# A transformer-SSD block on one core: more first products among the norms, a second bank for the states, other queues and places

## The chip, the cores and the metric

The kernel runs on one core of a Trainium2 chip. The metric is the device time in microseconds, here the median of three runs. Engines: TensorE (PE) multiplies, VectorE (DVE), ScalarE (ACT) and GpSimd (POOL) work on tiles, SyncE (SP) issues DMAs; ACT and POOL can issue DMAs too. Each has its own queue of instructions.

## The reference

One layer of depth 1 on 1024 tokens of width 1024, in fp32:

```python
f = swiglu(rmsnorm(h, ffn1_pre_g), ffn1_w_gate, ffn1_w_up, ffn1_w_down)   # d_ff 2816
h = h + 0.5 * rmsnorm(f, ffn1_post_g)
m = hybrid_mixer(rmsnorm(h, mix_pre_g))    # 8 heads of differential attention beside 16 heads of
h = h + rmsnorm(m, mix_post_g)             # a two-way Mamba-2 SSD (8 chunks of 128); one w_in, one w_out
f = swiglu(rmsnorm(h, ffn2_pre_g), ffn2_w_gate, ffn2_w_up, ffn2_w_down)
h = h + 0.5 * rmsnorm(f, ffn2_post_g)
return rmsnorm(h, final_g)
```

`swiglu(x)` is `(silu(x @ w_gate) * (x @ w_up)) @ w_down`. The SSD carries one state per group of heads from chunk to chunk: `state = state * decay + B^T (x dt decay)`.

## The kernel before

Every fp32 product is made of three matmuls (`mm3`, line 227): each operand is split into a high part (an ACT cast to the matmul's fp32 type) and a low part (the rest, by a DVE or POOL subtraction; `split`, line 223), and hi x hi, hi x lo and lo x hi are added in one PSUM bank.

The program is written in order, and the order of the instructions on each engine is chosen when it is built, from an estimate of when each is ready. In the chunks of the SSD PE's order is the written one, and in the attention that of PE, ACT, DVE and POOL.

*Gate and up (`blocks_gate_up`, line 368).* The two 1024 x 2816 products of a feed-forward are done in 2 x 2 blocks by a scheme with seven block products instead of eight. The 22 column tiles are taken in 11 pairs (i, i + 11). For a pair and a weight, `matrix` (line 420) loads two raw tiles, makes the sums s1 to s4 on POOL (lines 427 to 430), splits seven half tiles (`unit`), and runs seven `product`s of 12 matmuls (line 386) against the blocks b11, b21, b22, t1 to t4 of the normed tokens. C11 = a11 b11 + a12 b21 is one of the four results, and its first half a11 b11 (called u) enters the other three.

*The beginning of a feed-forward.* `blocks_prep` (line 323) prepares one row tile t of 128 tokens: a square sum on ACT, two small POOL steps (lines 253, 254), a scaling on DVE (line 330), for t >= 4 the sums t1 to t4 with the row tile t - 4 on POOL and DVE (lines 345 to 348), and turns: four PE transposes into one bank, then the split (ACT cast, DVE subtraction). Tiles 0 to 3 give b11 and b21, tiles 4 to 7 give b22, t1, t2, t3 and t4. Only when tile 7 is turned can a product with t2 begin; products with b11 and b21 can begin after tile 3. So `early` runs some of them among the norms: `begun` (line 399) does both products of C11 for gate and up of pair 0 in banks 4 and 5 and keeps u in SBUF, `held` (line 410) does a11 b11 of pair 1 in banks 6 and 7. `matrix` takes over what they left. In the first feed-forward `early` stands at line 1421, raw tiles have three places and split tiles six; in the second at line 1563, among the last rounds of the output projection, with two places each until `grow`.

*The chunks (`ssd_chunks`, line 811).* In chunk c, at step k = 1, the states of the two groups are made by `ssd_state` (line 782): three matmuls into the bank "st", then an addition to sf on DVE (line 792). Between the groups and between all steps stands `next(fill)`: 12 matmuls of the projections of q, k and v (`proj_heads`). Bank "pt" takes the transposes of the finished chunk c - 1 at k = 2 (`turn`, line 915). `decays` (line 852) multiplies dl and dr into two banks "pd"; `ssd_sums` (line 756) loads the rows of dl and dr, three DMAs for each of four groups of heads. For chunk 0 these loads follow the POOL selects of `ssd_rows` (line 754).

*The end of the heads.* Each half of a q or k tile is scaled and split into a tile o (`qk_store`, lines 981 and 982) and stored by SP (line 985); o has two places. After the chunks, the loads of the first attention head are issued on POOL (`attn_first`), the first w_out tile is loaded and split (`out_rounds`, by `unit`, lines 215 and 224), and the last eight steps of the heads run. The memory of that w_out tile was the chunks' before; the last chunk's rows (yT) are stored from it to mixT by ACT's queue (line 925).

Of the kernel before, what the change touches and what calls it, by code (L numbers as in the profile page):

```python
# [189 lines left out]
class Kernel:  # L190
    def __init__(self, ctx, tc, a):
# [6 lines left out]
        self.running, self.early = [], {}  # L198
# [124 lines left out]
    def blocks_prep(self, tags, x, y, ps, gain, C, t, junk=None):  # L323
# [44 lines left out]
    def blocks_gate_up(self, ring, cp, spool, ps, C, wg, wu, gd, early):  # L368
# [30 lines left out]
        def begun(i, banks):  # L399

            def one(r, b):
                p = ps.at(b, [P, 512], "b")
                u = spool.tile([P, 512], F32, tag="u", name="u", bufs=2)
                product(p, unit(r[:, 0:512], G), "b11")
                A.copy(out=u, in_=p)
                product(p, unit(r[:, 512:1024], G), "b21", True)
                first.append((u, p, b))
            return [lambda r=raw(w[i]), b=b: one(r, b) for w, b in zip((wg, wu), banks)]

        def held(i, banks):  # L410

            def one(w, b):
                r = ring.load(1024)[:, 0:512]
                nc.sync.dma_start(out=r, in_=w[i][:, 0:512])
                p = ps.at(b, [P, 512], "b")
                product(p, unit(r, G), "b11")
                first.append((None, p, b))
            return [lambda w=w, b=b: one(w, b) for w, b in zip((wg, wu), banks)]

        def matrix(w, i, final):  # L420
            u, p1, kept = first.pop(0) if first else (None, None, None)
            whole = u is None
# [8 lines left out]
            if not whole:  # L431
                final(i, 0, p1)
                ps.turn.append(kept)
            else:
                u = tile()
                if p1 is None:
                    p1 = bank()
                    product(p1, unit(a11), "b11")
                A.copy(out=u, in_=p1)
# [9 lines left out]
            if whole:  # L449
                product(p1, unit(a12), "b21", True)  # L450
                final(i, 0, p1)
                if kept is not None:
                    ps.turn.append(kept)
# [9 lines left out]
        early(begun, held)  # L463
# [318 lines left out]
    def ssd_state(self, ps, bt, xw, new, first, groups=(0, 1)):  # L782

        for g in groups:
            gs = slice(g * 512, (g + 1) * 512)
            bs = slice(g * P, (g + 1) * P)
            st = ps.tile([P, 512], F32, tag="st", name="st", bufs=1)
# [23 lines left out]
    def ssd_chunks(self, sp, ps, gain, fill):  # L811
# [125 lines left out]
        for s in range(N + 3):  # L937
# [30 lines left out]
            if k == 1 and c < T - 1:  # L968
                self.ssd_state(ps, C[c]["bt"], C[c]["xw"], self.sf, c == 0, (1,))
# [54 lines left out]

    def proj_v(self, ring, qp, ps, halves, g):

        w = [self.unit(ring, self.a["w_v"][g, i], 1024) for i in range(4)]
        for t in range(T):
# [7 lines left out]
            o = qp.tile([P, 2, 512], F32R, tag="o", name="o", bufs=2)  # L1036
# [6 lines left out]
    def proj_qk(self, ring, qp, ps, halves, pair):  # L1043

        for b in range(1, 4):
            w = self.unit(ring, self.a["w_qk"][3 * pair + b - 1], 1024)
            for half in range(2):
# [7 lines left out]
                self.qk_store(qp.tile([P, 2, 512], F32R, tag="o", name="o", bufs=2), p, pair, b, half)  # L1055
# [324 lines left out]
def build(tc, a, out, stages="all"):  # L1380
    nc = tc.nc
    with ExitStack() as top:
# [25 lines left out]
        k.gd = dr([NF, P, S], F32, name="gd")  # L1408
        with ExitStack() as c1:
            ps = Banks(k.pool(c1, "ps1", space=PSUM))  # L1410
            with ExitStack() as cb:
# [9 lines left out]
                def early(begun, held):  # L1421
# [9 lines left out]

                    ps.turn = [0, 1, 2, 3]
# [231 lines left out]
```

## Time and profile before

| | us |
|---|---|
| median of three runs | 2584.19 (2583.44 to 2584.79) |
| profiled execution | 2583.4 |
| its span, first to last instruction | 2581.6 |
| PE busy | 2474.8 |
| DVE busy | 1638.7 |
| ACT busy | 1099.4 |
| POOL busy | 971.7 |

The profile is that of one execution. Busy times are sums over the span; what an engine costs is read where PE stands still. A row of a timeline names start, duration, engine, line and operation, and in brackets how long the engine was idle before it and what ended that.

### The profile page before, as it was taken

The numbers are of one execution on the slowest core, as the hardware profiler recorded it, in microseconds if no ns is written. First come the engines' busy times: TensorE is split into PE (matmuls) and PEld (weight loads), VectorE is DVE, ScalarE is ACT, GpSimd is POOL, SyncE is SP. The second block draws the span as 40 slices with busy tenths as digits, with TensorE's granted clock in tenths as the row PEclk, the third lists the DMA queues.
The fourth block names the chain that finished last, engine by engine and source line by source line (L and its number), as shares of the span: only waits on it lengthen the run. The fifth ranks groups of instructions, "written<-read, shape, count | busy, mean of one in ns | idle before, by whom it ended". The sixth has DMA issues, their size and how long they took to land. (4 is left out here: it accounts for less than half of the span.)

```text
span 2581.6 us, 32800 instructions
## 1 busy us (share of the span) xinstructions
PE 2474.8 (96%) x11904; PEld 2063.1 (80%) x11904; DVE 1638.7 (63%) x2258; ACT 1099.4 (43%) x1899; POOL 971.7 (38%) x853
## 2 busy tenths in 40 slices
PE   6999999999999999999978999999889999999997
PEld 4888888888898889777766888888678888888886
DVE  7656555554746743677636888888875555555655
ACT  5332222343535533454426555555542223224443
POOL 7333231010220294244316666666673323310211
PEclk8999999999999999999999999999889999999999
DMA  4222222756732566465454444442332222227654
GB/s 148 89 74 90 90 74 83 232 182 201 246 121 91 169 214 229 161 198 185 149 163 110 123 119 119 110 122 84 123 102 94 82 86 78 82 91 267 228 167 153
DMA packets 156162, 356.79 MB, mean 138 GB/s; under 512 B 16224, under 2 KB 73696, under 8 KB 151136
## 3 DMA queue, kind: packets, MB, share of 16 engines
q1 hardware_dynamic: 137664, 293.09, 34.2%
q0 software_dynamic: 10016, 57.42, 8.3%
q10 hardware_dynamic: 8320, 4.19, 0.5%
q8 instruction: 94, 1.54, 0.3%
q14 instruction: 68, 0.56, 0.1%
HBM read 263.67 MB, written 90.96 MB: 137 GB/s over the span
## 5 line engine op out<-in xcount | busy, mean ns | idle before, releaser
L225 DVE TENSOR_TENSOR split<-raw,split 128x1024 fp32r<-128x1024 f32 (+3 forms) x223 | 256.1, 1156 | 101.9 <-ACT split L224 101.1
L224 ACT CAST split<-raw 128x512 fp32r<-128x512 f32 (+3 forms) x235 | 190.7, 825 | 191.6 <-issue 86.9
L1117 ACT ACTIVATE e<-sc,st 128x1024 f32<-128x1024 f32 x128 | 143.4, 1120 | 168.9 <-DVE st L1113 168.9
L230 PE MATMUL b<-hT,split 128*128 128x512 f32 x548 | 214.9, 393 | 0.0
L231 PE MATMUL b<-hT,split 128*128 128x512 f32 x548 | 214.3, 391 | 0.0
L232 PE MATMUL b<-hT,split 128*128 128x512 f32 x548 | 214.3, 391 | 0.0
L253 POOL TENSOR_SCALAR rstd<-rstd 128x1 f32<-128x1 f32 x64 | 28.3, 442 | 455.2 <-ACT junk L250 452.8
L231 PE MATMUL po<-split,gs 128*128 128x512 f32 x418 | 165.1, 395 | 0.0
L232 PE MATMUL po<-split,gs 128*128 128x512 f32 x418 | 165.1, 395 | 0.0
L230 PE MATMUL po<-split,gs 128*128 128x512 f32 x418 | 164.4, 395 | 0.0
L230 PE MATMUL pp<-hT,split 128*128 128x512 f32 x384 | 153.8, 400 | 10.4 <-DVE o L982 10.4
L1113 DVE TENSOR_REDUCE st<-sc 128x1 f32<-128x1024 f32 x128 | 150.5, 1217 | 12.6 <-PE sc L1111 12.6
L230 PE MATMUL b<-t,split 128*128 128x512 f32 x396 | 155.4, 392 | 0.1
L231 PE MATMUL b<-t,split 128*128 128x512 f32 x396 | 155.1, 392 | 0.0
L232 PE MATMUL b<-t,split 128*128 128x512 f32 x396 | 154.6, 391 | 0.0
L225 DVE TENSOR_TENSOR gs<-graw,gs 128x384 fp32r<-128x384 f32 (+1 forms) x126 | 70.3, 561 | 132.7 <-ACT gs L224 132.5
L232 PE MATMUL pp<-hT,split 128*128 128x512 f32 x384 | 152.0, 396 | 0.0
L231 PE MATMUL pp<-hT,split 128*128 128x512 f32 x384 | 151.7, 395 | 0.0
L427 POOL TENSOR_TENSOR s<-raw 128x512 f32<-128x512 f32 x31 | 43.6, 1406 | 284.5 <-DMA raw<-in_w_up_dram 143.8
L1124 POOL TENSOR_SCALAR e<-e,st 128x768 f32<-128x768 f32 x64 | 75.7, 1183 | 186.7 <-DVE st L1123 143.0
L224 ACT CAST gs<-graw 128x384 fp32r<-128x384 f32 (+1 forms) x126 | 59.4, 474 | 188.8 <-PE po L232 166.1
L224 ACT CAST split<-s 128x512 fp32r<-128x512 f32 x101 | 60.9, 620 | 142.4 <-PE b L232 131.0
(427 smaller groups left out, 7124.1 us busy)
## 6 DMA issues: line engine op xcount, KB each, us to landing
raw<-in_w_down_dram SPq DMA_DIRECT2D x93, 512.0 KB
acc<-in_w_down_dram SPq DMA_DIRECT2D x39, 512.0 KB
raw<-in_w_gate_dram SPq DMA_DIRECT2D x34, 512.0 KB
raw<-in_w_up_dram SPq DMA_DIRECT2D x32, 512.0 KB
qkd<-o SPq DMA_DIRECT2D x64, 256.0 KB
qk<-qkd POOLq DMA_DIRECT2D x16, 1024.0 KB, 7.8
graw<-gd SPq DMA_DIRECT2D x82, 192.0 KB
gd<-w SPq DMA_DIRECT2D x43, 256.0 KB
```

The lines of the kernel that those rows point to most:

```text
L224: self.nc.scalar.copy(out=hi, in_=src)
L225: (eng or self.nc.vector).tensor_tensor(out=lo, in0=src, in1=hi.bitcast(F32), op=ALU.subtract)
L230: mm(out=out, lhsT=a[0], rhs=b[0], start=start, stop=False, **kw)
L231: mm(out=out, lhsT=a[0], rhs=b[1], start=False, stop=False, **kw)
L232: mm(out=out, lhsT=a[1], rhs=b[0], start=False, stop=stop, **kw)
L253: nc.gpsimd.tensor_scalar(out=r[:, 1:2], in0=r[:, 0:1], scalar1=k / n, scalar2=k * EPS, op0=ALU.mult, op1=ALU.add)
L427: G.tensor_tensor(out=s1, in0=a21, in1=a22, op=ALU.add)
L1113: nc.vector.tensor_reduce(out=X["st"][:, j:j + 1], in_=pc, op=ALU.max, axis=AX.X, negate=True)
L1117: self.nc.scalar.activation(out=X["e", j], in_=X["sc", j], func=AF.Exp, bias=st[:, j:j + 1], accum_out=st[:, 2 + j:3 + j])
L1124: G.tensor_scalar(out=e1[:, XD:], in0=e1[:, XD:], scalar1=st[:, 5:6], scalar2=0.0, op0=ALU.mult, op1=ALU.add)
```

## The change

In both feed-forwards `held` goes, and `begun` does the whole of C11 for pairs 0, 1 and 2: gate and up each with b11 and b21, then silu, multiplication and store. Its u goes to DRAM (`ud`) from POOL's queue, and `matrix` loads it back on SP. In `blocks_prep` the tags in `low` get their low part otherwise: after ACT's cast, PE adds the cast times a negative identity (`minus`) to the transposes' bank, and ACT copies what is left. Those tags are t2, t3, t4 in the first feed-forward and all but b22 in the second. The second group's state uses bank "pt". The dr loads of chunk 0 are issued by ACT. For the last four tiles of the heads, o alternates between its two places and two of the output projection's "odd" tiles.

```diff
+    def new_minus(self, tile):
+        self.minus = tile
+        self.nc.scalar.activation(out=tile, in_=self.ident, func=AF.Copy, scale=-1.0)
...
+    def blocks_prep(self, tags, x, y, ps, gain, C, t, junk=None, low=()):
...
-                nc.tensor.transpose(out=pt[:, i, :], in_=s[:, i * P:(i + 1) * P], identity=self.ident)
-            self.split(pt, C[n][0][:, :, ts], C[n][1][:, :, ts])
+                nc.tensor.matmul(out=pt[:, i, :], lhsT=s[:, i * P:(i + 1) * P], rhs=self.ident, is_transpose=True,
+                                 start=n not in low or i == 0, stop=n not in low or i == 3, skip_group_check=n in low)
+            hi, lo = (c[:, :, ts] for c in C[n])
+            if n in low:
+                nc.scalar.copy(out=hi, in_=pt)
+                nc.tensor.matmul(out=pt, lhsT=self.minus, rhs=hi, start=False, stop=True, skip_group_check=True)
+                nc.scalar.copy(out=lo, in_=pt)
+            else:
+                self.split(pt, hi, lo)
...
         def begun(i, banks):
...
+            ps2 = [ps.at(b, [P, 512], "b") for b in banks]
+            def one(m, w):
+                r = raw(w[i])
                 u = spool.tile([P, 512], F32, tag="u", name="u", bufs=2)
+                product(ps2[m], unit(r[:, 0:512], G), "b11")
+                A.copy(out=u, in_=ps2[m])
+                nc.gpsimd.dma_start(out=ud[2 * i + m], in_=u)
+                product(ps2[m], unit(r[:, 512:1024], G), "b21", True)
+                first.append(2 * i + m)
+            def out():
+                sg = gate11(ps2[0], spool.tile([P, 512], F32, tag="s", name="s", bufs=3))
+                V.tensor_tensor(out=sg, in0=sg, in1=ps2[1], op=ALU.mult)
+                store(sg, i, 0)
+            return lambda: one(0, wg), lambda: one(1, wu), out
...
         def matrix(w, i, final):
+            done = first.pop(0) if first else None
...
+            u = tile()
+            if done is None:
+                p1 = bank()
+                product(p1, unit(a11), "b11")
+                A.copy(out=u, in_=p1)
             else:
+                nc.sync.dma_start(out=u, in_=ud[done])
...
     def ssd_sums(self, c, k):
         dma = self.nc.sync.dma_start
+        right = self.nc.scalar.dma_start if c == 0 else dma
...
-        dma(out=self.dr[32 * k:32 * k + 2].bitcast(F32), in_=src)
+        right(out=self.dr[32 * k:32 * k + 2].bitcast(F32), in_=src)
...
-                    self.ssd_state(ps, C[c]["bt"], C[c]["xw"], self.sf, c == 0, (0,))
+                    self.ssd_state(ps, C[c]["bt"], C[c]["xw"], self.sf, c == 0, (0,), ("st", "pt"))
...
+    def new_o(self, qp):
+        self.os.append(self.os.pop(0))
+        if self.os[-1] is None:
+            return qp.tile([P, 2, 512], F32R, tag="o", name="o", bufs=2)
+        return self.os[-1].tile([P, 2, 512], F32R, tag="odd", name="o", bufs=2)
...
+        k.os = [None, None, wo, wo]
         H = k.attn_first(hp)
```

`early` of the first feed-forward, from tile 4 on (`step` runs one stage of `blocks_prep`):

```diff
-                    gate, up = begun(0, (4, 5))
                     xs += [load(t) for t in (4, 5, 6)]
                     step(4)
                     step(4)
+                    gate, up, out = begun(0, (4, 5))
                     gate()
                     step(5)
+                    step(4)
                     up()
-                    for t in (4, 5, 6, 5, 6):
-                        step(t)
-                    gate, up = held(1, (6, 7))
+                    step(6)
+                    step(5)
+                    step(5)
+                    out()
+                    gate, up, out = begun(1, (6, 7))
                     gate()
+                    step(6)
                     step(7)
                     step(6)
                     up()
                     step(7)
+                    out()
+                    gate, up, out = begun(2, (4, 5))
+                    gate()
                     step(7)
+                    up()
+                    out()
```

`early` of the second, after the last row tile is pushed:

```diff
                 up()
                 k.move()
-                gate, up = held(1, (6, 7))
+                out()
+                gate, up, out = begun(1, (6, 7))
                 gate()
                 k.move()
                 up()
+                out()
                 k.finish()
+                gate, up, out = begun(2, (4, 5))
+                gate()
+                up()
+                out()
```

## Rows read from the trace of the kernel before

**Rows 1.** The page, part 1: busy time of each engine, share of the span, instructions.
```profile
PE 2474.8 (96%) x11904; PEld 2063.1 (80%) x11904; DVE 1638.7 (63%) x2258; ACT 1099.4 (43%) x1899; POOL 971.7 (38%) x853
```

**Rows 2.** Waits of PE, whole span: line <- releaser: us in total, times, longest.
```profile
PE pp L230 <- DVE o L982: 10.4, 1, 10.4
...
PE st L230 <- DVE sf L792: 9.2, 4, 2.4
...
PE pd L856 <- DMA qkd<-o: 4.2, 1, 4.2
...
PE pd L856 <- ACT dd L860: 3.4, 5, 0.7
```

**Rows 3.** Stretches: length, busy PE, PEld, DVE, ACT, POOL (instructions), clock, DMA share, GB/s.
```profile
18.74:41.30 22.56, 22.56 (x113) 18.47 (x112) 13.70 (x16) 9.72 (x18) 21.90 (x21) 0.93 0.32 105
...
41.30:63.98 22.68, 10.29 (x42) 7.60 (x41) 22.55 (x24) 12.82 (x24) 16.94 (x13) 0.60 0.22 70
...
1836.00:1868.74 32.74, 23.11 (x93) 16.91 (x93) 28.27 (x38) 15.62 (x30) 21.39 (x24) 0.84 0.43 150
...
1868.74:1895.80 27.06, 27.06 (x135) 22.09 (x134) 23.38 (x24) 14.54 (x27) 22.86 (x20) 0.94 0.43 148
...
1895.80:1912.70 16.90, 8.73 (x38) 7.08 (x36) 16.46 (x20) 9.93 (x20) 15.42 (x12) 0.60 0.37 120
```

**Rows 4.** Timeline in a chunk (start, duration, engine, line, [idle before]): PE and DVE.
```profile
1159.28 0.39 PE L232 MATMUL pp<-hT,split 128*128 128x512 f32 x1
...
1161.33 0.68 DVE L792 TENSOR_TENSOR sf<-sf,st 128x512 f32<-128x512 f32 x1
...
1162.66 0.63 PE L231 MATMUL st<-xw,bt 128*128 128x512 f32 x1
...
1163.09 0.63 PE L232 MATMUL st<-xw,bt 128*128 128x512 f32 x1
```

**Rows 5.** Timeline at the first chunk's start: POOL, SP's queue and PE.
```profile
1029.36 3.12 POOL L754 TENSOR_SCALAR_AFFINE_SELECT dr<-dr 32x1024 fp32r<-32x1024 f32 x2
...
1034.07 0.25 SPq L760 DMA_DIRECT2D dr<-csT  x1
...
1037.05 1.19 PE L856 MATMUL pd<-dr,dl 128*128 128x512 f32 x2 [4.25 <-DMA qkd<-o]
```

**Rows 6.** Timeline at the end of the heads: ACT.
```profile
1345.43 1.04 ACT L224 CAST even<-raw 128x1024 fp32r<-128x1024 f32 x1 [17.57 <-DMA raw<-in_w_out_dram]
...
1346.38 1.26 ACT L981 ACTIVATE o<-pp,qscale 128x512 fp32r<-128x512 f32 x2
```

**Rows 7.** Waits of SP's queue, 1300 to 1370.
```profile
SPq L215 <- DMA mixT<-yT: 19.7, 1, 19.7
```

**Rows 8.** Timeline at the first feed-forward: PE.
```profile
39.73 1.04 PE L336 MATMUL pt<-ident,w 128*128 128x128 f32 x8
...
45.74 1.09 PE L336 MATMUL pt<-ident,w 128*128 128x128 f32 x4 [4.30 <-DVE hT L225]
...
67.88 0.39 PE L230 MATMUL b<-hT,split 128*128 128x512 f32 x1
...
70.60 0.39 PE L230 MATMUL b<-t,split 128*128 128x512 f32 x1
```

**Rows 9.** Groups by line, 18.74 to 64, POOL: count | busy us, mean ns | idle.
```profile
L225 POOL TENSOR_TENSOR split<-raw,split 128x512 fp32r<-128x512 f32 x4 | 5.4, 1364 | 0.1
...
L427 POOL TENSOR_TENSOR s<-raw 128x512 f32<-128x512 f32 x3 | 4.2, 1412 | 3.9 <-DMA raw<-in_w_gate_dram 3.9
```

**Rows 10.** Line 668's DMA issues on POOL, 960 to 1012: ns min/median/max.
```profile
L668 POOL DMA_DIRECT2D szd<-z x14: 540/542/607, 959.6 to 1011.6; - x14
```

**Rows 11.** Groups by line, 18.74 to 64, DVE and ACT.
```profile
L225 DVE TENSOR_TENSOR t<-pt,t 128x512 fp32r<-128x512 f32 x10 | 6.5, 677 | 0.0
...
L224 ACT CAST t<-pt 128x512 fp32r<-128x512 f32 x11 | 6.3, 591 | 12.4 <-PE pt L336 12.4
...
L250 ACT ACTIVATE junk<-w 128x1024 bf16<-128x1024 f32 x3 | 3.2, 1061 | 2.0 <-DMA w<-in_x_dram 2.0
```

More of the change, by code (lines that the diff above doesn't have):

```diff
@@ L366, in half_units, with blocks_gate_up @@
         return unit
-    def blocks_gate_up(self, ring, cp, spool, ps, C, wg, wu, gd, early):
+    def blocks_gate_up(self, ring, cp, spool, ps, C, wg, wu, gd, ud, early):
         nc = self.nc
@@ L399, in begun @@
         def begun(i, banks):
-            def one(r, b):
-                p = ps.at(b, [P, 512], "b")
+            ps2 = [ps.at(b, [P, 512], "b") for b in banks]
+            def one(m, w):
+                r = raw(w[i])
                 u = spool.tile([P, 512], F32, tag="u", name="u", bufs=2)
[L404 to L418, printed above, removed]
+                product(ps2[m], unit(r[:, 0:512], G), "b11")
[8 more added lines that the diff above has]
+            return lambda: one(0, wg), lambda: one(1, wu), out
         def matrix(w, i, final):
-            u, p1, kept = first.pop(0) if first else (None, None, None)
-            whole = u is None
+            done = first.pop(0) if first else None
             r0, r1 = raw(w[i]), raw(w[i + 11])
@@ L430, in matrix @@
             G.tensor_tensor(out=s4, in0=a12, in1=s2, op=ALU.subtract)
-            if not whole:
-                final(i, 0, p1)
-                ps.turn.append(kept)
-            else:
[L435 to L439, printed above, removed]
+            u = tile()
[3 more added lines that the diff above has]
+                A.copy(out=u, in_=p1)
+            else:
+                nc.sync.dma_start(out=u, in_=ud[done])
             p6, p5, p7 = bank(), bank(), bank()
@@ L448, in matrix @@
             final(i + 11, 1, c22)
-            if whole:
+            if done is None:
                 product(p1, unit(a12), "b21", True)
                 final(i, 0, p1)
-                if kept is not None:
-                    ps.turn.append(kept)
             product(p5, unit(s4), "b22", True)
@@ L462, in blocks_gate_up @@
         first = []
-        early(begun, held)
+        early(begun)
         for i in range(NF // 2):
@@ L780, in ssd_weigh, with ssd_state @@
         return xw
-    def ssd_state(self, ps, bt, xw, new, first, groups=(0, 1)):
+    def ssd_state(self, ps, bt, xw, new, first, groups=(0, 1), tags=("st", "st")):
         for g in groups:
@@ L786, in ssd_state @@
             bs = slice(g * P, (g + 1) * P)
-            st = ps.tile([P, 512], F32, tag="st", name="st", bufs=1)
+            tag = tags[g]
+            st = ps.tile([P, 512], F32, tag=tag, name=tag, bufs=1)
             self.mm3(st, (bt[:, 0, bs], bt[:, 1, bs]), (xw[:, 0, gs], xw[:, 1, gs]), True, True)
@@ L1035, in proj_v @@
                 self.mm3(p, (H[:, 0, d, ts], H[:, 1, d, ts]), (w[d // 2][:, 0, ws], w[d // 2][:, 1, ws]), d == 0, d == 7)
-            o = qp.tile([P, 2, 512], F32R, tag="o", name="o", bufs=2)
+            o = self.new_o(qp)
             self.split(p, o[:, 0, :], o[:, 1, :])
@@ L1054, in proj_qk @@
                     self.mm3(p, (w[:, 0, ds], w[:, 1, ds]), (H[:, 0, d, :], H[:, 1, d, :]), d == 0, d == 7)
-                self.qk_store(qp.tile([P, 2, 512], F32R, tag="o", name="o", bufs=2), p, pair, b, half)
+                self.qk_store(self.new_o(qp), p, pair, b, half)
                 yield
@@ L1430, in load @@
                         return x
+                    k.new_minus(zp.tile([P, P], F32R, tag="z", name="minus", bufs=3))
                     ps.turn = [0, 1, 2, 3]
@@ L1442, in step @@
                         if t == len(prep):
-                            prep.append(k.blocks_prep(tags, xs[t], kept[t - 4], ps, g, C, t, junk))
+                            prep.append(k.blocks_prep(tags, xs[t], kept[t - 4], ps, g, C, t, junk, ("t2", "t3", "t4")))
                         next(prep[t], None)
@@ L1463, in early @@
                     step(7)
+                    out()
+                    gate, up, out = begun(2, (4, 5))
+                    gate()
                     step(7)
-                k.blocks_gate_up(ring, tags, spool, ps, C, a["w_gate1"], a["w_up1"], k.gd, early)
+                    up()
+                    out()
+                    ps.turn = [6, 7, 0, 1, 2, 3, 4, 5]
+                k.blocks_gate_up(ring, tags, spool, ps, C, a["w_gate1"], a["w_up1"], k.gd, ud, early)
             nrm, gains = norm_pools(c1)
@@ L1561, in build, with early @@
             C = k.blocks(*k.new_halves())
-            def early(begun, held):
+            def early(begun):
+                k.new_minus(rp.tile([P, P], F32R, name="minus"))
                 ps.turn = [0, 1, 2, 3]
@@ L1573, in early @@
                             C[n] = [pool.tile([P, 4, 512], F32R, tag=x, name=n, bufs=1 if pool is hp else 2) for x in tags]
-                        gate, up = begun(0, (4, 5))
+                        gate, up, out = begun(0, (4, 5))
                         gate()
                     k.push(k.residual(nrm, acc[t], t, h1, g2["mix"], 1.0, h2, nc.gpsimd if t < 4 else nc.vector,
-                                      lambda f, x, t: k.blocks_prep(nrm, f, acc[t - 4], ps, g2["pre"], C, t)))
+                                      lambda f, x, t: k.blocks_prep(nrm, f, acc[t - 4], ps, g2["pre"], C, t, None, ("b11", "b21", "t1", "t2", "t3", "t4"))))
                 up()
                 k.move()
-                gate, up = held(1, (6, 7))
+                out()
+                gate, up, out = begun(1, (6, 7))
                 gate()
```

11 lines of the change are left out of this document (6 added, 5 removed).

## Prediction

> **What bounds the kernel now.** The page's first part comes first: TensorE (PE) is busy 2474.8 of 2581.6 us [rows 1], so an engine other than PE matters only where PE stands still, and all of it that can be won is 106.8 us. The second view is PE's waits: who ended each idle stretch. Three entries belong to the mixer [rows 2]: one of 10.4 us, four that sum to 9.2 us, one of 4.2 us. The third view is the table of stretches, read at the two places where a feed-forward begins and token rows are normed, turned and split [rows 3]. There PE is idle for 22.68 - 10.29 = 12.4 us (41.3 to 63.98) and 16.9 - 8.73 = 8.2 us (1895.8 to 1912.7) at a granted clock of 0.60, which means that much of it ran at the lower level, 1.2 GHz. In both, DVE is the engine that is full: 22.55 of 22.68 and 16.46 of 16.9 us. Behind these two stretches PE has no gap, so work that moves into them is taken off the end.
>
> **Profiled run and median.** The profiled execution took 2583.4 us for a span of 2581.6. The median of the three runs is 2584.19, 0.8 above it. The sum is made on the span, and its difference is then taken off the median.
>
> **State of the second group.** The chunk's first state matmuls write the one bank "st"; the second group's wait until DVE has added the first (line 792). PE's last matmul before the wait starts at 1159.28, DVE reaches the addition only at 1161.33, behind other work, and the stall reads 2.40 us in the list of waits [rows 2, 4]. In the bank "pt" the second group needs none of this: the bank's other user, the transposes of the chunk before, comes a whole fill (12 matmuls) and more later, and by then the addition of the second group is done. So 9.2 us go. After a stall the next matmuls stand 0.43 us apart instead of 0.23 [rows 4, 8], some seven of them in the worst of the four, near 2 us in all. What is late next is the pair "pd", which already waits 0.7 us for ACT five times [rows 2]; PE that comes earlier may wait there more, up to 0.7 us in each of seven chunks (4.9). I take **9**, bounds 4 to 11.
>
> **First sums.** The four dr loads of chunk 0 leave SP's queue for ACT's. The last POOL select ends at 1029.36 + 3.12 = 1032.48, SP issues the last load at 1034.07, PE starts at 1037.05 [rows 5]. Only the 1.6 us between select and issue belong to a queue; the 3.0 us to PE's start are the transfer and stay. New is that ACT now waits for POOL: behind such a load in ACT's order stand evictions of q and k (line 981), whose bank PE needs next. If the last load falls behind one of them it is later than now by as much. I take **1**, bounds -3 to 4.2 (the whole stall). The Trainium skill (Trainium Kernel Development and Optimization, Key Constraints) says that DMAs issued by SP, ACT and POOL share the same engines and that several issuers save only issue time. By it, the gain could not pass 1.6 of the 4.2 us, where a reading of the stall as "SP is crowded" would give 4.2.
>
> **Four places for q, k and v.** The list is set just before the last head steps, so only the last four o tiles see it: two of them still use the old places, two the new ones. The 10.4 us wait is for the eviction of such a tile. But ACT does that eviction at 1346.38, right behind the cast of the first w_out tile, which ended its own wait only at 1345.43 [rows 6]. That tile's load sat on SP for 19.7 us until the store mixT<-yT had left the place [rows 7]. Nothing in this chain is an o tile, and the change moves neither cast nor load. So I take **0**; the bounds are 0 and 10.4 plus a restart at 0.43 us for about eleven matmuls, 12.6.
>
> **C11 of three pairs, first feed-forward.** Before, six products (12 matmuls each) ran among the norms: four of pair 0 and two of pair 1. After, twelve do, and the six leave the stretch behind. One product is 70.60 - 67.88 = 2.72 us [rows 8], so 16.3 us are moved. The lower halves of t2, t3 and t4 no longer cost DVE 0.68 us each [rows 11]: PE subtracts with a negative identity (one 512-column matmul, 0.23 us and a change of weights: 0.3 by estimate) and ACT copies a second time, 0.59 [rows 11]. For 4 tokens x 3 that is 3.6 us more on PE, 7.1 more on ACT and 8.1 less on DVE. Room on PE between 18.74 and 63.98: 12.4 us idle, and nine groups of four transposes that take some 0.9 us where eight take 1.04 at the full clock [rows 8], 9 x 0.45 = 4.1; together 16.5. Wanted: 16.3 + 3.6 = 19.9. So the point at which matrices begin moves from 63.98 to 67.4 and what follows is 16.3 shorter: 12.9 us. This asks that PE is never without work. DVE gets free, since its splits for the matrices can follow later. POOL is the tight one: busy 21.9 + 16.9 = 38.8 of 45.2 us now [rows 3], of which some nine sums for matrices (lines 427 to 430) of about 1.4 each [rows 9], 13 in all, may come later; it gains six unit splits of 1.36 [rows 9] and six DMA issues of 0.54 [rows 10], 11.4 us, and fits. The issue of a u store waits on POOL for ACT's copy of u, and token sums (lines 345 to 348) queue behind. The low-part matmul waits for ACT's first copy, with products queued behind it on PE. I leave 2 us for these waits: **11**, bounds 2 and 14. The reload of u on SP waits for a place of tag "c"; raw loads queue behind it, but DMA is busy a quarter of the time there [rows 3]; 0.
>
> **The same, second feed-forward.** Six tags are low here: 8 turns of b11 and b21, 16 of t1 to t4. From 1868.74 to 1912.7 there are 8.2 us idle and eight slow groups of transposes, at the 0.45 of the first beginning 3.6: 11.8. Wanted: 16.3 + 16 x 0.3 = 21.1. The start moves by 9.3, so 7.0 are won. Before it, from 1836, PE is idle 9.6 us while DVE is busy 28.3 of 32.7 [rows 3]; eight halves leave DVE there (5.4 us), of which I count 2. POOL has 38.3 of 44 us and the same 11.4 on top, with fewer sums to put off; ring places are two instead of three. I leave 3 us for waits: **6**, bounds -4 and 12.4 (7.0 + 5.4).
>
> **Sum.** 9 + 1 + 0 + 11 + 6 = 27: span 2554.6, and 2584.2 - 27 = 2557 for the median.
>
> **Rivals.** *POOL takes over from DVE.* In the first stretch 38.8 + 11.4 = 50.2 us of work, and about 1 us for each of six stores that wait for u, give a start at 18.74 + 56 = 75 instead of 67: 5 us won; in the second about 2. With 10 from the mixer: 2567. For it speaks that POOL was full from 18.74 to 41.3 [rows 3]; against it, the sums that can wait.
>
> *The stall of the heads goes too.* If the program's order puts the tile's eviction ahead of the cast, up to 12.6 us more: 2544. Against it stands the chain [rows 6, 7].
>
> *The added low matmul holds PE up.* PE now waits for ACT inside its own queue, 36 times. The nearest row is pd, which waits 0.7 us for an ACT copy [rows 2]. If a Square of the norms (1.06 [rows 11]) lies ahead of each first copy, 36 x 1.06 = 38 us are lost, where my sum without its 5 us for waits has 32 to give: 2590, **slower**. It decides from 32 / 36 = 0.9 us per place. Against it: PE has slack in both stretches, and ACT is busy 12.8 of 22.7 and 9.9 of 16.9 us [rows 3]. The Trainium skill (TensorE: Matmul & The Clock Gate, Step-by-step: what each phase is for) says that matmuls keep their program order and only weight loads are pulled ahead; by that rule no product can pass a waiting low matmul, and this rival is possible at every place. Between 0.75 and 1.03 us per place the time is the old one, 2584.
>
> *The change doesn't do what it says:* in the order that is built the extra products land behind the norms instead of among them. Then the two feed-forwards give nothing and 2574 is left.
>
> **How the numbers follow.** Chances: forecast 49%, POOL 18%, heads' stall gone 15%, low matmul slower 7%, low matmul about even 7%, products not among the norms 4%. About 0.2% (5 us) is what a measurement of this kernel can tell from no change. Faster: 49 + 18 + 15 + 4 = 86%; within: 7%; slower: 7%. Range 2542 to 2575: it takes in the rival with the heads and POOL, and leaves out the two cases of the low matmul and some of the tails.
>
> **What would show it.** Right: no wait st <- sf; a product pitch without gaps from about 19 to 67 us; DVE well under full there; PE's idle total down by over 25 us. Wrong, by step: pt <- ACT among PE's waits of about 1 us (low matmul); POOL at 95% and more with PE idle (POOL); pp <- o gone (heads); new waits at pd or at the transposes pt in the chunks. The prediction is wrong above all if the two beginnings, 17 of the 27 us, behave otherwise.

## The result and the profile after

The median after is 2569.47 us (2565.52 to 2572.04, four runs) against 2584.28 before on the same chip (2583.44 to 2584.79). The ratio is 0.9945 (95% interval 0.9933 to 0.9956): 14.8 us less, clear of the scatter, where 27 were forecast. The profiled execution took 2572.04 us, the longest of the four, for a span of 2570.3.

The page's part 1, and PE's waits over the whole span (line <- releaser: us in total, times, longest), answer to [rows 1, 2]:

```profile
PE 2478.0 (96%) x11940; PEld 2062.7 (80%) x11940; DVE 1612.5 (63%) x2210; ACT 1117.7 (43%) x1937; POOL 997.5 (39%) x877
...
PE pp L230 <- DVE o L989: 10.0, 1, 10.0
...
PE pd L863 <- DMA qkd<-o: 7.4, 1, 7.4
...
PE po L230 <- ACT qk L224: 4.6, 1, 4.6
...
PE yo L230 <- DVE dd L868: 3.7, 4, 1.4
...
PE po L231 <- DVE qk L225: 3.5, 1, 3.5
PE pd L863 <- ACT dd L867: 3.4, 5, 0.7
```

The waits of the state bank `st` are gone. The heads' stall (`pp`) is as it was. The first sums' stall (`pd` for a DMA) has grown from 4.2 to 7.4, and there are two waits at `po` with no counterpart in [rows 2]: they are in the second down projection, a stage of which the prediction says nothing.

PE's timeline gives the marks from which stages can be compared. Before (the row of the first sums is in [rows 5]):

```profile
1348.44 0.80 PE L230 MATMUL pp<-hT,split 128*128 128x512 f32 x1 [10.43 <-DVE o L982]
...
1836.39 0.41 PE L336 MATMUL pt<-ident,acc 128*128 128x128 f32 x2 [1.51 <-DVE vv L1178]
...
2327.34 0.62 PE L230 MATMUL po<-split 128*128 128x512 f32 x2
```

After:

```profile
1032.70 0.77 PE L863 MATMUL pd<-dr,dl 128*128 128x512 f32 x1 [7.39 <-DMA qkd<-o]
...
1333.55 0.79 PE L230 MATMUL pp<-hT,split 128*128 128x512 f32 x1 [10.00 <-DVE o L989]
...
1821.35 0.41 PE L341 MATMUL pt<-ident,acc 128*128 128x128 f32 x2 [1.52 <-DVE vv L1192]
...
2307.26 0.80 PE L230 MATMUL po<-qk,split 128*128 128x512 f32 x1 [4.58 <-ACT qk L224]
...
2503.84 0.80 PE L231 MATMUL po<-qk,gs 128*128 128x512 f32 x1 [3.53 <-DVE qk L225]
```

Each row is the first matmul after a stall or of a stage (2327.34 is the first of the second step of the down projection; after, that step was due at 2307.26 - 4.58 = 2302.68). Differences of the marks give the table; E3 and E5 are two of the experiments below.

| stage, us on PE | before | after | E3 | E5 |
|---|---|---|---|---|
| start to arrival at the first sums | 1032.80 | 1025.31 | 1024.72 | 1024.60 |
| stall of the first sums | 4.25 | 7.39 | 5.56 | 6.50 |
| chunks | 300.96 | 290.85 | 290.22 | 290.20 |
| heads' stall | 10.43 | 10.00 | 9.85 | 1.80 |
| last heads, attention | 487.95 | 487.80 | 488.03 | 485.81 |
| second norms, gate and up, first step of down | 490.95 | 481.33 | 481.17 | 481.35 |
| rest of the second down projection | 254.26 | 267.62 | 254.85 | 254.84 |
| span | 2581.6 | 2570.3 | 2554.4 | 2545.1 |

So the first feed-forward won 7.5, the chunks 10.1 and the second feed-forward 9.6 us. The first sums lost 3.1, and the second down projection lost 13.4. The table compares single executions, which lie 11.3 us apart, the medians 14.8: some 3.5 us of what it adds up to are scatter between executions. PE's arrival at the first sums, for one, lies between 1024.02 and 1025.31 us in kernels with the same first feed-forward.

The stretches of [rows 3], the last three moved by the 15 us that PE is earlier there (length, busy PE, PEld, DVE, ACT, POOL, clock, DMA share, GB/s):

```profile
18.74:41.30 22.56, 21.50 (x93) 17.41 (x92) 11.14 (x14) 14.27 (x27) 22.36 (x18) 1.00 0.32 105
41.30:63.98 22.68, 22.68 (x119) 18.73 (x118) 8.05 (x8) 12.33 (x24) 18.86 (x19) 1.00 0.50 163
1821.00:1853.74 32.74, 26.85 (x113) 18.95 (x114) 27.31 (x33) 21.16 (x41) 22.74 (x25) 0.95 0.53 180
1853.74:1880.80 27.06, 25.22 (x125) 20.26 (x124) 19.08 (x16) 16.15 (x30) 22.62 (x24) 1.00 0.42 147
1880.80:1897.70 16.90, 16.90 (x91) 14.11 (x90) 5.27 (x5) 10.93 (x22) 13.65 (x13) 1.00 0.66 232
```

The two stretches that ran at a clock of 0.60 have no idle time now and a clock of 1.00. DVE, full before, is busy 8.05 of 22.68 and 5.27 of 16.90 us. POOL is at 99% and 83% in the first beginning, and PE does not wait for it. PE's idle time over the whole span fell from 106.8 to 2570.3 - 2478.0 = 92.3 us, by 14.5 and not by the 25 and more that the prediction had named as a sign.

### The profile page after: what moved, and what is told of

Its sections match the earlier page's. It is cut to its first block, busy times and chain, and to the rows that moved or that the text cites. A ratio compares the mean times of both kernels' runs of the same rounds, so it can differ in the third digit from the quotient of the medians.

```text
span 2570.3 us, 32871 instructions
## 1 busy us (share of the span) xinstructions
PE 2478.0 (96%) x11940; PEld 2062.7 (80%) x11940; DVE 1612.5 (63%) x2210; ACT 1117.7 (43%) x1937; POOL 997.5 (39%) x877
## 4 chain that ended last, share of the span: by engine, by line
PE 80%; DVE 7%; ACT 4%; POOL 4%; DMA 3%; issue 2%; SPq 0%; DVEq 0%; ACTq 0%; POOLq 0%
PE b L231 11%; PE b L232 11%; PE b L230 11%; PE po L231 7%; PE po L230 7%; PE po L232 7%; PE pp L230 5%; PE pp L231 5%; PE pp L232 5%; PE pgu L230 2%; PE pgu L232 2%; PE sc L1125 2%; PE sc L1124 2%; PE pgu L231 2%; ACT e L1131 1%
## 5 line engine op out<-in xcount | busy, mean ns | idle before, releaser
L225 DVE TENSOR_TENSOR split<-raw,split 128x1024 fp32r<-128x1024 f32 (+3 forms) x217 | 244.6, 1133 | 104.0 <-ACT split L224 99.4
L230 PE MATMUL b<-hT,split 128*128 128x512 f32 x556 | 219.0, 395 | 1.2 <-DVE w L452 1.2
L231 PE MATMUL b<-hT,split 128*128 128x512 f32 x556 | 218.7, 393 | 0.8 <-ACT hT L347 0.5
L232 PE MATMUL b<-hT,split 128*128 128x512 f32 x556 | 218.1, 393 | 0.9 <-POOL split L225 0.9
L253 POOL TENSOR_SCALAR rstd<-rstd 128x1 f32<-128x1 f32 x64 | 33.6, 525 | 451.9 <-ACT junk L250 449.6
L231 PEld LDWEIGHTS b<-hT,split 128*128 128x128 f32 x556 | 105.0, 189 | 23.9 <-DVE hT L225 0.9
```

What stands on the lines that cost most here:

```text
L225: (eng or self.nc.vector).tensor_tensor(out=lo, in0=src, in1=hi.bitcast(F32), op=ALU.subtract)
L230: mm(out=out, lhsT=a[0], rhs=b[0], start=start, stop=False, **kw)
L231: mm(out=out, lhsT=a[0], rhs=b[1], start=False, stop=False, **kw)
L232: mm(out=out, lhsT=a[1], rhs=b[0], start=False, stop=stop, **kw)
L253: nc.gpsimd.tensor_scalar(out=r[:, 1:2], in0=r[:, 0:1], scalar1=k / n, scalar2=k * EPS, op0=ALU.mult, op1=ALU.add)
```

## Experiments

Each comes with the edit. A ratio is to the kernel before, run on the same chip, where its median was 2583.22 us for E1 to E4, 2583.59 for E5 to E8 and 2583.70 for E9; in a diff, lines with - are of the kernel named. The expectations call the five terms of the prediction's sum steps (a) to (e): (a) the first sums, (b) the state, (c) the four places, (d) and (e) the first and the second feed-forward.

**E1: the state's bank alone**, in the kernel before.

```diff
-            st = ps.tile([P, 512], F32, tag="st", name="st", bufs=1)
+            st = ps.tile([P, 512], F32, tag=tags[g], name=tags[g], bufs=1)   # tags ("st", "pt") in the chunks
```

> The kernel before with one edit: the second group's state product goes into the transposes' bank. Forecast by my step (b): the waits of the second group's state for the first group's addition (9.2 us in four places, at `st`) go, and the start of the heads' stall, 1338.01 us before, comes 9 us earlier (7 to 11); the median falls by 9 to 10 us, to about 2575. Rival: in the changed kernel the chunks got faster (10.1 us between the first sums and the heads' stall) because the first sums and the chunk loads moved, not because of the bank; then the bank alone gives under 4 us, and the median stays above 2580. A second rival: the state waits in its new bank for the transposes' evictions instead, and DVE's additions hold `yo` up; then the waits at `pt` and `yo` grow by as much as those at `st` shrink.

Measured: 2577.42 us (2576.2 to 2580.36), ratio 0.9977 (0.9967 to 0.9988). PE's timeline:

```profile
1036.38 0.77 PE L856 MATMUL pd<-dr,dl 128*128 128x512 f32 x1 [4.21 <-DMA dr<-csT]
...
1337.09 0.80 PE L230 MATMUL pp<-hT,split 128*128 128x512 f32 x1 [10.25 <-DVE o L982]
...
1900.69 0.47 PE L336 MATMUL pt<-ident,acc 128*128 128x128 f32 x1 [4.55 <-POOL acc L345]
```

The chunks take 1337.09 - 10.25 - 1036.38 = 290.46 us, 10.5 less than before: the bank alone makes the whole gain, and the first rival falls. The second one is there in small: `yo` waits 3.7 us. But only 5.8 us reach the median. 5.7 are lost some 560 us later, in the second feed-forward, which holds the same instructions in another order: on POOL the weights' sums (lines 427 to 429, 1893.76 to 1898.96) now stand ahead of a token sum (line 345), for which PE waits 4.55 us. Before, that token sum ran at 1903.88 with the weights' sums behind it.

**E2: the first sums' loads back on SP**, in the changed kernel.

```diff
-        right = self.nc.scalar.dma_start if c == 0 else dma
+        right = dma
```

> The changed kernel with the first sums' four loads put back on SP's queue. Theory: in the changed kernel ACT's queue is what holds the first sums up: ACT stood 6.25 us at the first of these loads and then 8.69 us at an eviction that waited for a store, with the third and fourth load behind it, so that PE's stall there grew from 4.25 to 7.39 us. Back on SP the stall is 4 to 5.5 us, and the median falls by 2 to 3 us, to about 2567. Rival: what holds the loads up is POOL's preparation of the same tile, which ends at 1024.0 us, and the loads and stores in SP's own queue; then the stall stays at 7 us or grows, and the median doesn't fall.

Measured: 2569.19 us (2566.86 to 2570.19), ratio 0.9938 (0.9925 to 0.9952): no change from the changed kernel's 2569.47. The timelines, first of the changed kernel (ACT and its queue), then of this one (SP's queue and PE):

```profile
1015.80 0.69 ACT L988 ACTIVATE o<-pp,qscale 128x512 fp32r<-128x512 f32 x1 [6.25 <-POOL dr L759]
...
1027.80 0.69 ACT L988 ACTIVATE o<-pp,qscale 128x512 fp32r<-128x512 f32 x1 [8.69 <-DMA qkd<-o]
1027.83 2.66 ACTq L766 DMA_DIRECT2D dr<-csT  x2
```

```profile
1024.85 0.80 SPq L992 DMA_DIRECT2D qkd<-o  x2
1026.19 0.25 SPq L766 DMA_DIRECT2D dr<-csT  x1
...
1030.78 0.76 PE L863 MATMUL pd<-dr,dl 128*128 128x512 f32 x1 [6.76 <-DMA dr<-csT]
```

My theory falls. On ACT the last two loads stand behind an eviction that waits for a store; on SP they stand behind the stores themselves, and the stall is 6.76 us. With the loads on ACT and the same first feed-forward, six other profiles (E3 to E6, E8, E9) start the first sums between 1029.42 and 1031.75 us, the changed kernel itself at 1032.70. No run shows one queue to be the better one.

**E3: the halves of the shared tile together**, in the changed kernel.

```diff
-            self.splits += [lambda t=t: self.wo.tile(...) for t in ("odd", "odd", "even", "even")]
+            self.splits[3:3] = [lambda t=t: self.wo.tile(...) for t in ("odd", "odd", "even", "even")]
```

> The changed kernel with one edit in the second down projection: the four new places for split weights are put into the ring ahead of the last place, so that the two halves of the shared tile `qk` follow one another in the ring, the new tile first, as they did before the change. Theory: three early pairs take 6 whole places where before one pair and a product each of two took 3, so the ring stands at an odd point when the down projection begins; the second half of one tile and the first half of the next are then two places apart, and the next tile has to wait until the last product of the old half has run. That is the cause of both new stalls, 4.58 us at 2307.26 and 3.53 us at 2503.84. Both go, and the median falls by 6 to 9 us, to about 2562. Rival: the loads of the gate's last results come too late because the last matrices end earlier than their loads can follow; then PE stalls at the start of the down projection as long as before, on `gs` in place of `qk`, and the median falls by under 3 us.

Measured: 2556.57 us (2555.86 to 2557.35), ratio 0.9893 (0.9879 to 0.9906), 12.9 us less than the changed kernel where 6 to 9 were expected. No wait at `po` is left in the down projection. Two stretches of it, the changed kernel first:

```profile
2300.00:2340.00 40.00, 35.42 (x145) 28.40 (x144) 19.54 (x22) 17.03 (x22) 0.00 (x0) 0.91 0.84 291
2500.00:2540.00 40.00, 36.47 (x147) 29.34 (x146) 27.53 (x32) 17.21 (x27) 8.12 (x6) 0.91 0.66 228
```

```profile
2300.00:2340.00 40.00, 40.00 (x175) 32.52 (x174) 22.16 (x25) 18.44 (x24) 0.00 (x0) 1.00 0.87 317
...
2500.00:2540.00 40.00, 39.81 (x173) 32.03 (x171) 21.08 (x29) 14.76 (x28) 0.93 (x3) 1.00 0.44 156
```

The stalls cost more than their 8.1 us: with each the granted clock falls (0.91 in the mean of the stretch), and the rest of the down projection is 267.62 - 254.85 = 12.8 us longer. What the first stall looked like on ACT in the changed kernel:

```profile
2301.65 0.51 ACT L224 CAST gs<-graw 128x384 fp32r<-128x384 f32 x1 [5.29 <-DMA graw<-gd]
2303.57 0.51 ACT L224 CAST gs<-graw 128x384 fp32r<-128x384 f32 x1 [1.41 <-DMA graw<-gd]
2304.80 1.04 ACT L224 CAST even<-raw 128x1024 fp32r<-128x1024 f32 x1 [0.72 <-DMA raw<-in_w_down_dram]
2305.76 0.51 ACT L224 CAST gs<-graw 128x384 fp32r<-128x384 f32 x1
2306.17 1.04 ACT L224 CAST qk<-acc 128x1024 fp32r<-128x1024 f32 x1
```

PE needs the last of these, the weights of the second step, and ACT has it behind the casts of the third step and later ones, which wait for loads. In E3 these same `graw` casts wait as long (5.21 us at 2299.21), and nobody misses them: the rival, late loads, falls as the cause. At the second stall it is DVE that is late: ACT's cast of that `qk` tile began at 2496.67 us, but DVE's subtraction only at 2502.56, behind a step of the norms (line 296, 2501.36).

**E4: two places for q, k and v**, in the changed kernel: the line `k.os = [None, None, wo, wo]` is left out.

> The changed kernel without the two further places for q, k and v (the line that names their pools is left out, so that all use the two of before). Forecast by my step (c): no change, within 1 us of 2569.5; the heads' stall, 10.00 us with four places and 10.43 before, is 10 to 10.5. Rival: the places are what brings the 1338.01 us mark forward, with evictions that no longer wait for stores; then the heads' stall starts later or grows by more than 2 us, and the median rises by as much.

Measured: 2571.69 us (2569.16 to 2572.31), ratio 0.9948 (0.9936 to 0.9961).

```profile
1332.03 0.79 PE L230 MATMUL pp<-hT,split 128*128 128x512 f32 x1 [9.74 <-DVE o L989]
...
1844.47 0.47 PE L341 MATMUL pt<-ident,acc 128*128 128x128 f32 x1 [3.80 <-DVE acc L1384]
```

The heads' stall is the same without the places, and it starts no later, so the rival falls. The median is 2.2 us higher where 1 was allowed, but the executions of the two kernels overlap. What differs is again the second feed-forward, in another order: 485.17 us to the end of the first step of down, where the changed kernel takes 481.33. On DVE, ACT and POOL the traces show one order there in the changed kernel, E2, E3 and E5, and one other in E4 and E8, with the same instructions.

**E5: the cast that held ACT up goes to POOL**, on top of E3.

```diff
-        ws = [[weights(0, 0)]] + [[] for _ in range(R)]
+        raw, sp = rings[0].load(1024), rings[0].take(1024)
+        nc.sync.dma_start(out=raw, in_=self.a["w_out"][8])
+        nc.gpsimd.tensor_copy(out=sp[:, 0, :], in_=raw)
+        nc.gpsimd.tensor_tensor(out=sp[:, 1, :], in0=raw, in1=sp[:, 0, :].bitcast(F32), op=ALU.subtract)
+        ws = [[sp]] + [[] for _ in range(R)]
```

> The kernel of the run with the halves together (2556.57 us) with one more edit: the first weights of the output projection are split by POOL in place of ACT and DVE. Theory: what holds the heads' stall (9.85 us there) is the order of ACT's queue alone: the cast of these weights stands ahead of two evictions and waits 17 us for a load that waits for the last mixed tile's store. POOL is idle in that stretch. With the cast gone from the queue the evictions run, the stall falls under 3 us, and the median falls by 6 to 10 us, to about 2548. Only then can the two further places for q, k and v be worth something, as the stores stand in SP's queue behind the same load. Rival: the stores behind the load in SP's queue hold the places, the further places lie in memory that is itself waiting for that store, and the stall is as long as before; then the median stays at 2556 to 2557.

Measured: 2547.29 us (2546.84 to 2547.59), ratio 0.9861 (0.9844 to 0.9877). This is the fastest kernel of the study, 36 us below the one before. ACT's timeline in E3, then ACT and PE in E5:

```profile
1327.33 1.04 ACT L224 CAST even<-raw 128x1024 fp32r<-128x1024 f32 x1 [16.98 <-DMA raw<-in_w_out_dram]
1328.28 1.26 ACT L988 ACTIVATE o<-pp,qscale 128x512 fp32r<-128x512 f32 x2
```

```profile
1321.58 1.27 ACT L988 ACTIVATE o<-pp,qscale 128x512 fp32r<-128x512 f32 x2 [10.42 <-DMA qkd<-o]
...
1323.10 0.50 PE L230 MATMUL pp<-hT,split 128*128 128x512 f32 x1 [1.80 <-DVE o L989]
```

The cast in front was the cause: without it the stall is 1.80 us. (The edit takes the subtraction from DVE too, but the rows show ACT as the engine that was held up.) In its place a second wait shows, for a store of q or k (10.42 us), and most of it is covered. Why these stores, and that of the last mixed tile, were so slow is not tested. The trace suggests the loads of the first attention head: POOL issued five of them from 1301.64 to 1303.77 us, the last took 18.7 us to land where 5.5 is the median of its line, and the DMA engines were full (length, busy PE, PEld, DVE, ACT, POOL, clock, DMA share, GB/s):

```profile
1310.00:1322.00 12.00, 11.30 (x50) 9.01 (x48) 0.75 (x1) 1.11 (x2) 0.00 (x0) 1.00 1.04 285
```

That ACT's queue never lets a later instruction pass is what the Trainium skill says (PSUM — Partial Sum Buffer, Engine vs sequencer instructions: a strict FIFO); the 16.98 us of E3's cast, ahead of two evictions, agree.

**E6: two early pairs in the second feed-forward**, in the changed kernel, its ring left as the change has it.

```diff
-                gate, up, out = begun(2, (4, 5))
-                gate()
-                up()
-                out()
-                ps.turn = [6, 7, 0, 1, 2, 3, 4, 5]
+                ps.turn = [4, 5, 0, 1, 2, 3, 6, 7]
```

> The changed kernel with two early pairs in the second feed-forward in place of three; the ring in the second down projection is left as the change has it. Two pairs take 4 whole places, so the ring then stands at an even point, with the halves of the shared tile side by side. Theory of the halves: both stalls of the second down projection (4.58 and 3.53 us) and the low clock behind them are gone without any other edit, and, since the third pair runs only when the norms are done and so fills no gap, nothing is lost: the median is about 2557, like the run with the halves together. Rival: the stalls come from the three pairs' later loads or from PE arriving earlier; then they go only as far as PE arrives later, and the median stays within 4 us of 2569.

Measured: 2563.36 us (2561.89 to 2564.72), ratio 0.9922 (0.9908 to 0.9937). One half of the expectation held: no wait at `po` of 0.7 us or more in the down projection, which takes 254.64 us after its first step, without any edit of the ring. The other half failed: the third pair is worth 7.1 us in its own stage (488.26 against 481.17 in E3). The order that is built puts its products between the last turns of the norms. Without them PE meets this (DVE, then PE):

```profile
1885.58 5.06 DVE L225 TENSOR_TENSOR split<-s,split 128x512 fp32r<-128x512 f32 x1 [0.47 <-ACT split L224]
...
1891.98 0.45 PE L341 MATMUL pt<-ident,acc 128*128 128x128 f32 x1 [4.20 <-DVE hT L225]
```

**E7: DVE's subtractions back in the first feed-forward**, on top of E3: `low` is left at its default there.

> The kernel of the run with the halves together (2556.57 us) with DVE's subtractions back in the first feed-forward's norms: the twelve low halves of the sums are made by DVE at 0.68 us each, and the twelve matmuls with the negative identity (about 0.5 us each on PE) go. Theory (my step (d)): DVE is what PE waited for beside the norms, 22 us of work in the 45 us with the gaps, so the gaps come back in part and the median rises by 2 to 6 us, to 2559 to 2563. Rival: the products of three pairs cover DVE's work in any case, and the twelve matmuls are only added PE work of 6 us in all; then the median falls, by up to 6 us, to 2551 to 2556.

Measured: 2560.7 us (2559.67 to 2560.96), ratio 0.9912 (0.9897 to 0.9926). The time is the theory's, the mechanism is not: no gap comes back among the norms. PE is idle there as little as in E3 (21.51 and 22.68 busy), DVE is far from full, and the first product with t2 begins at 66.23 us, 2.3 us earlier than in E3 (68.48). So far the rival is right: the products of three pairs cover DVE's work. E7's stretches (length, busy PE, PEld, DVE, ACT, POOL, clock, DMA share, GB/s):

```profile
18.74:41.30 22.56, 21.52 (x97) 17.46 (x97) 13.49 (x17) 14.46 (x27) 22.36 (x18) 1.00 0.34 105
41.30:63.98 22.68, 22.68 (x124) 19.09 (x123) 10.58 (x17) 9.66 (x20) 18.89 (x20) 1.00 0.55 180
```

The loss comes later. At 109.05 us PE waits 3.97 for an addition on DVE, at the end of a chain that goes back over ACT to the sums on POOL, the first of which waited 5.16 us for a raw tile's load. PE arrives at the first sums at 1033.92 - 7.48 = 1026.44, 1.7 us later than in E3. The stall there is 1.9 longer, and the second feed-forward, in another order once more, takes 1.4 more (2304.31 - 1821.69 = 482.62 against 481.17).

```profile
109.05 0.80 PE L230 MATMUL b<-hT,split 128*128 128x512 f32 x1 [3.97 <-DVE w L452]
...
1033.92 0.77 PE L863 MATMUL pd<-dr,dl 128*128 128x512 f32 x1 [7.48 <-DMA qkd<-o]
```

**E8: two places on top of E5**, by the edit of E4.

> As the run with the cast by POOL, without the two further places for q, k and v. If the further places come into their own once the cast no longer blocks ACT's queue, the heads' stall is longer here than there, by 3 to 10 us, since two evictions find both places waiting for stores that stand behind a load in SP's queue. If the places were never the limit, both runs agree within 1 us.

Measured: 2553.98 us (2550.61 to 2554.71), ratio 0.9884 (0.9869 to 0.9898). Neither expectation held. The heads' stall is 2.43 us against 1.80, and the stage behind it 1.1 longer, so the places are not the limit; but the kernel is 6.7 us slower by the medians and 3.7 by the profiled executions. In the profile the second feed-forward takes 3.9 us more (485.29 against 481.35), with the order of E4 and the same gap:

```profile
1832.95 0.47 PE L341 MATMUL pt<-ident,acc 128*128 128x128 f32 x1 [3.78 <-DVE acc L1388]
```

**E9: DVE's subtractions back in the second feed-forward**, on top of E5.

> The kernel of the run with the cast by POOL (2547.29 us) with DVE's subtractions back in the second feed-forward's norms: 24 low halves by DVE at 0.68 us each, and 24 matmuls with the negative identity less on PE. Theory (my step (e), which left DVE as the engine that PE waits for there): the gaps among the norms come back, and the median rises by 4 to 12 us, to 2551 to 2559. Rival: as in the first feed-forward, the three pairs are what counts and the subtraction is worth little: the median stays within 2 us of 2547. A second rival: the 24 matmuls cost PE more than they free, and the median falls.

Measured: 2552.9 us (2551.96 to 2554.92), ratio 0.9881 (0.9864 to 0.9897). The time is the first theory's: 5.6 us more by the medians, 5.2 in the stage (486.51 against 481.35). The mechanism is so only in part. PE, then ACT:

```profile
1840.06 0.48 PE L341 MATMUL pt<-ident,acc 128*128 128x128 f32 x1 [3.82 <-DVE hT L225]
...
1893.03 0.79 PE L230 MATMUL b<-hT,split 128*128 128x512 f32 x1 [5.00 <-ACT u L419]
```

```profile
1891.88 0.62 ACT L224 CAST qk<-raw 128x512 fp32r<-128x512 f32 x1 [5.48 <-DMA raw<-in_w_gate_dram]
1892.40 0.58 ACT L419 COPY u<-b 128x512 f32<-128x512 f32 x1
```

The wait of 3.82 us is for DVE, and the kernel before has the same one (3.82 at 1866.95). The longer one is not: PE waits for ACT's copy of u, which stands on ACT behind a cast that waits for a load, the pattern that E5 removed at the heads; DVE is idle for 8.15 us until 1892.53. The turns end earlier than in E5 (1882.75 against 1891.46 us), and most of the third pair runs behind them. How much of the 5.2 us is DVE's subtraction, and how much the other order, stays open.

## Why the prediction was half right

The range held the time, and the sign was right. The likeliest value, 2557, was 12 us too low, and not because of a term of the sum: the five terms together gave 7.5 - 3.1 + 10.1 + 0.4 + 9.6 = 24.5 of the 27. What failed is the step that stopped at the stages the change names: it put the second down projection at nothing, without a word, and there 13.4 us were lost. With this one cost taken out (E3) the kernel takes 2556.57 us. That this is so near 2557 is luck in part: the terms were off by +1.1, -4.1, +0.4, -3.5 and +3.6, in the order of the sum, and these nearly cancel.

**State of the second group**, 9 forecast: 10.1 in the changed kernel, 10.5 alone (E1). The wait is gone as described. What is late next is `yo` (3.7 us for DVE's `dd`) and not `pd`, whose five waits stay at 3.4.

**First sums**, 1 forecast, lower bound -3: the stage lost 3.1 in the profiled run, 1.3 in E3. The step took the end of this stall as moving with PE's arrival; it did not. Of the 7.5 to 8.8 us that PE arrives earlier, the start of the first sums follows by 4.3 to 7.6, with the loads on either queue (E2). That ACT would now wait for POOL, and evictions behind it, was seen rightly (6.25 us), but it costs no more than SP's queue did. The rule of the Trainium skill that the step cites (Trainium Kernel Development and Optimization, Key Constraints), that several issuers save only issue time, agrees: the queue made no difference that the medians show.

**Four places**, 0 forecast: 0.4 in the heads' stall, and the chain that was named is the cause (E5). What the step could not see is that the line also changes the order that is built for the second feed-forward: kernels without it lose 3.8 and 3.9 us there (E4, E8). So the edit is worth something, through an effect far from the stage it was made for.

**First feed-forward**, 11 forecast: 7.5, or 8.1 in E3. The sum there was 12.9 less 2 for waits. The first product with t2 began at 68.66 us where 67.4 was forecast (1.3), and DVE's additions held PE up for 1.6 at 95.22 and 98.60; that leaves 10.0, and PE is in fact 9.9 us ahead at the 288th product matmul (104.18 us after, 114.12 before). Of this lead 1.7 us go evenly over the rest of gate and up, where the matmuls stand 227.7 ns apart in the mean against 226.7 before (200 to 380 us), and 0.8 behind it; why is open. Most of the gain is the pairs'. The step's other half, DVE's relief, was not needed among the norms (E7): without the matmuls that subtract PE is done with them 2.3 us earlier, and what E7 loses, 1.7 us, it loses at a later wait.

**Second feed-forward**, 6 forecast, upper bound 12.4: 9.6. The 3 us that I left for waits were not needed: in the last stretch PE has no idle time at all. Without the third pair the stage is 7.1 longer (E6), without the subtraction by PE 5.2 (E9), in both with another order that has a part in it.

**Rivals.** POOL as the next bound: not seen, though POOL was at 99%. The low matmul that holds PE up: one of the 36 waits, 0.40 us at 1825.01, and two products wait 0.4 and 0.5 for ACT's second copy, where 0.9 at all 36 would have decided. The heads' stall stayed, as the forecast had it.

**What was missed.** The second feed-forward takes 77 whole places of the ring of split weights for gate and up. The three early pairs take six of them while the ring still has two places, where before three were taken; that leaves 71 for the ring of four, where it was 74 before and is 73 in E6. Two of the ring's four places are halves of one tile (`qk`). Before, the ring stood at an even point when the down projection began: both halves, then both other places. Now it stands at an odd point: second half, two others, first half of the next tile. Two facts are shown: with the halves put together again both stalls go (E3), and with two pairs, which leave the ring even, they go as well (E6). Each run changes something else too. E3 also brings the four new places forward; but the second stall goes as well, and it lies 200 us on, where no place is new any more. In E6 PE arrives 7 us later; but in E3 it arrives as early as in the changed kernel. Why an odd ring stalls is argued from the code: the next tile has to wait for the products of both old halves, one of which has just been handed out as the operand of the first step, so the order that is built puts its cast late, behind casts that wait for loads, or its subtraction late on DVE. A count of places up to the next stage would have shown the odd point, though hardly its 13 us.

## What to carry to other kernels

When an edit changes how many places of a rotating ring are used, count on to the next stage that takes from the same ring, above all where several places share one tile. When the order of instructions is chosen at build time, an edit in one stage can cost 1 to 6 us in another with the same instructions (E1, E4, E7, E8): compare stages by marks on the critical engine, not whole times. For an in-order queue, look for an instruction that waits for a slow transfer and has short, urgent ones behind it; moving that one elsewhere (E5) was worth 9.3 us. And look where a forecast that came true got its time from: E7, and E9 in part, met their ranges by waits that their theories did not name.

## What the runs showed of the hardware

A DVE subtraction of two operands in SBUF (128x512) took 5.06 us in E6, where the same form takes 0.68 at 1892.52 in the same profile. Through those 5.06 us POOL ran four additions and subtractions of 1.26 to 1.28 us back to back (lines 357, 437, 438 and 359, 1885.14 to 1890.09), and DVE ended 0.55 us behind the last of them. The Trainium skill describes such a lock (SBUF — State Buffer, SBUF: two separate sides: DVE, with two operands in SBUF, and POOL share a pair of ports, and one blocks the other for a whole instruction). The row agrees, and adds that DVE did not get in between POOL's instructions here. So the order of POOL's work can stop PE although POOL itself is not what PE waits for, as in the 4.20 us of E6.

A stall of 4.58 us cost more than itself: the step of 18 matmuls behind it took 6.31 us (2307.26 to 2313.57) where the next took 4.08, at a granted clock of 0.65 in the mean, so for much of it at the lower level, 1.2 GHz. The six of line 230 took 656 ns in the mean, the six of line 231 476, where 392 is usual in the same stretch. Rows of the changed kernel: the step's stretch, and groups from 2302 to 2325 us (count | busy us, mean ns | idle):

```profile
2307.26:2313.57 6.31, 6.31 (x19) 5.00 (x19) 2.59 (x3) 0.90 (x1) 0.00 (x0) 0.65 1.03 412
...
L230 PE MATMUL po<-even,gs 128*128 128x512 f32 x11 | 4.3, 392 | 0.0
L230 PE MATMUL po<-qk,split 128*128 128x512 f32 x6 | 2.9, 656 | 4.6 <-ACT qk L224 4.6
L231 PE MATMUL po<-qk,split 128*128 128x512 f32 x6 | 2.9, 476 | 0.0
```
